# Six joined edits to a fused attention, mLSTM and GLA layer: opening, value products, first output sums, y splits, last tile, weight buffers

## The chip, the core and the metric

The kernel runs on one core of a Trainium2 chip. TensorE (PE in the rows, PEld for its weight loads) multiplies into PSUM banks, VectorE (DVE), ScalarE (ACT) and GpSimd (POOL) work element by element, and SyncE (SP) issues nearly all DMAs. The metric is the device time of one execution in microseconds, the median of the runs.

## What is computed

One layer over 2048 tokens of width 1024, in fp32. `h` is the RMS norm of `x`; one input projection feeds three head groups, whose gated outputs are concatenated and projected back, with a residual and a final RMS norm:

```
hn = rmsnorm(x, norm_g);  z = hn @ w_in        # split into aq ak av ag | mq mk mv mo mi mf mg | gq gk gv ga gg
y_a = band_chunk_attention(aq, ak, av, rel_bias) * silu(ag)     # 6 heads of 64, own 64-chunk + 8 previous
y_b = sigmoid(mo) * head_rmsnorm(mlstm(conv(mq), conv(mk), mv, mi, mf)) * silu(mg)     # 6 heads of 64
y_c = head_rmsnorm(gla(gq, gk, gv, log_alpha(ga))) * silu(gg)   # 4 heads, keys 32, values 64
out = rmsnorm(x + concat(y_a, y_b, y_c) @ w_out, final_g)
```

## The kernel before, in words

Every large product is made of fp32r operands split in two: `hi` is the value rounded by a ScalarE copy (line 237 for weights, 332 for `x`, 997 for `y`), `lo` the rest by a subtraction on VectorE or GpSimd (238, 333, 998); three matmuls (hi hi, hi lo, lo hi) make one product. The 2048 tokens go in four quarters of 512.

**The opening.** `prep_x` (283) loads the quarter's `x` token by token, squares it with a row sum on ScalarE, and makes diagonal tiles `dg` of the norm factors; `prep` (297) multiplies them by ones on TensorE (302) so that the factors stand along the free axis, copies them to SBUF (`rbs`, 304), loads `xT` (feature-major `x`), scales it in place on VectorE (311), and multiplies the small gate weights `wg` (318). `split_x` (326) makes the eight `X` tiles. Only then does the first projection `proj_z` (436, matmuls at 245 to 247) start.

**Phase A.** Per quarter: `proj_z` (gq, gk), `proj_t` (258, values, token-major), gg, mq/mk with a convolution, mo/mg, and the nine attention projections; between them stand the pieces of the mLSTM (`mlstm`), of GLA (`gla_in`, `gla`) and of the gates. TensorE's order is the program's, written by a planner (`Flow`) with estimated gaps; the other engines' and SP's orders come from the framework's scheduler. Weight tiles `w` are split from raw loads in two `wraw` buffers into a ring of five. Attention's q, k, v and gates and the finished mLSTM and GLA outputs go to DRAM (`q_d`, `k_d`, `v_d`, `ga_d`, `y_d`). Of the last quarter's attention projections six tiles are kept back (`kept`).

**Phase B.** `attention0` runs the first quarter's six heads: `scores` (936; matmuls at 960, `pt` the probabilities) and `mix` (1001). It runs beside the kept projections. `load_wo` splits the output weights and loads and splits the first quarter's `y` tiles 3 to 7. In `mix` the probabilities of each pair of 128-token tiles are transposed (1032) in packs of up to 512 columns, split into `ph` and `pl` (1037, 1038), and multiplied with the values `vv` (1046 hi, 1049 lo), two packs behind; the sum in the one bank `w` goes to `cc` (1052, 1053), and after each second head `split_y` makes y tiles 0 to 2. Then, for quarters 1 to 3, `attention(q)` is merged with `out_mm(q - 1)` (1088; matmuls 1099 to 1101, order of the y tiles 3, 4, 5, 6, 7, 0, 1, 2); the quarter's y tiles 3 to 7 come back from DRAM by `load_y` (1119). `out_mm(3)` runs alone at the end, and each of its tiles ends in residual add, square sum, gain, norm factor and store (1104 to 1116).

Of the kernel before, what the change touches and what calls it, by code (L numbers as in the profile page):

```python
# [8 lines left out]
FP32 = mybir.dt.float32  # L9
# [18 lines left out]
G0 = 96  # L28

# [46 lines left out]
def merge(a, b, na, nb):  # L76
    acc = 0
# [27 lines left out]
def trunk_kernel(ctx: ExitStack, tc: tile.TileContext, xT, x, w_f, w_t, w_o, w_gates, norm_g, conv_w,  # L105
# [34 lines left out]
    wring = pg_.enter_context(tc.tile_pool(name="wring", bufs=5))  # L140
# [3 lines left out]
    with ExitStack() as pa_:  # L144
# [13 lines left out]
        def d_tile():  # L158
# [18 lines left out]
        zr = d_tile()  # L177
        nc.gpsimd.memset(zr, 0.0)
        nc.vector.tensor_copy(hl_nm, zr.rearrange("p h t -> p (h t)")[:, 0:QT])
        nc.vector.tensor_copy(hl_iw, zr[:, 0, 0:NC])  # L180
        nc.gpsimd.affine_select(out=zr[0:32], in_=zr[0:32], pattern=[[-1, 6], [0, P]], compare_op=ALU.not_equal,
                                fill=1.0, base=0, channel_multiplier=1)
        nc.scalar.copy(zr[32:64], zr[0:32])
        nc.scalar.copy(zr[96:128], zr[0:32])
        nc.vector.memset(zr[0:32], 0.0)
        nc.vector.tensor_copy(sel, zr)
# [33 lines left out]
        def load_consts():  # L220
            nc.sync.dma_start(wg[:, :, 0:28], w_gates)
            nc.sync.dma_start(onerow, one_row)
            nc.sync.dma_start(gsel, gate_sel)
# [6 lines left out]

        def load_w(src, k):
            w = wring.tile([P, 2 * D], FR, name="w").rearrange("p (k l n) -> p k l n", k=k, l=2)
# [8 lines left out]
        def proj_g(name, X, out_, per):  # L241
            w = load_w(w_f[_F.index(name)], KT)
# [40 lines left out]
        def prep_x(q):  # L283
            t0 = q * QT
            rs = big.tile([P, NC], FP32, name="rs")
            for tt in range(NC):
                xt = xraws.tile([P, D], FP32, name="xraw")
                nc.sync.dma_start(xt, x[t0 + tt * P:t0 + (tt + 1) * P, :])
                nc.scalar.activation(xt, xt, AF.Square, accum_out=rs[:, tt:tt + 1])
# [7 lines left out]
        def prep(q, R, dg):  # L297
# [26 lines left out]
            R["raws"], R["g1"] = raws, g1  # L324

# [11 lines left out]
        def gates(q, g1, R):  # L337
# [26 lines left out]
            nc.scalar.copy(hl_nm[G0:G0 + MH], nm)  # L364
# [12 lines left out]
            nc.scalar.copy(hl_iw[G0:G0 + MH], il)  # L377
# [136 lines left out]
        def proj_kept(X):  # L514
            for b, name in kept:
                out_ = []
                yield from proj_g(name, X, out_, 1)
                att_in(NQ - 1, X, b, out_[0])

        def bias_rel():  # L520
            bc = big.tile([P, AH], FP32, name="sm")
            nc.sync.dma_start(bc, bias[:, :, 256])
            for p in range(AH // 2):
                b2 = g_tile([P, QT]).rearrange("p (h j) -> p h j", h=2)
                nc.sync.dma_start(b2, bias[:, 2 * p:2 * p + 2, 0:256])
                for h in range(2):
                    nc.gpsimd.tensor_scalar(b2[:, h, :], b2[:, h, :], bc[:, 2 * p + h:2 * p + h + 1], None, op0=ALU.subtract)
# [701 lines left out]
```

## Time and profile before

| what | value |
|---|---|
| median of 3 runs | 1318.02 us (1317.06 to 1320.14) |
| profiled execution | 1321.42 us, of it 1319.7 us span from first to last instruction |
| TensorE busy | 1266.8 us, 96% of the span |
| VectorE, ScalarE, GpSimd busy | 813.0, 595.9, 630.6 us |
| mean granted TensorE clock | 0.982 |

Busy time of TensorE counts overlapping matmuls once, and a matmul that runs at half clock is as busy as one at full clock, so 96% does not say how much is left. What is left shows as waits of TensorE and as stretches of granted clock 0.5. In the timeline a matmul's own duration is longer than its share of the stream; its price is the distance from its start to the next one's.

### The profile page before, as it was taken

The numbers are of one execution on the slowest core, as the hardware profiler recorded it, in microseconds if no ns is written. First come the engines' busy times: TensorE is split into PE (matmuls) and PEld (weight loads), VectorE is DVE, ScalarE is ACT, GpSimd is POOL, SyncE is SP. The second block draws the span as 40 slices with busy tenths as digits, with TensorE's granted clock in tenths as the row PEclk, the third lists the DMA queues.
The fourth block names the chain that finished last, engine by engine and source line by source line (L and its number), as shares of the span: only waits on it lengthen the run. The fifth ranks groups of instructions, "written<-read, shape, count | busy, mean of one in ns | idle before, by whom it ended". The sixth has DMA issues, their size and how long they took to land.

```text
span 1319.7 us, 19935 instructions
## 1 busy us (share of the span) xinstructions
PE 1266.8 (96%) x7044; PEld 1038.1 (79%) x7044; DVE 813.0 (62%) x1859; ACT 595.9 (45%) x1124; POOL 630.6 (48%) x847
## 2 busy tenths in 40 slices
PE   4999999999999999999999999999979999999997
PEld 2788777878787788877778787887768888889876
DVE  7626656672775767267666866664467767666711
ACT  5624422463443247244224543332466556556621
POOL 5327652332766225367622656642165454454442
PEclk7999999999999999999999999999889999999999
DMA  7444233634423354442244333328677656565222
GB/s 249 157 120 136 84 104 113 181 121 138 129 80 106 111 183 133 127 134 86 91 127 125 112 102 88 108 69 260 180 221 218 184 176 187 157 206 148 81 95 79
DMA packets 106516, 181.66 MB, mean 138 GB/s; under 512 B 9776, under 2 KB 54704, under 8 KB 106416
## 3 DMA queue, kind: packets, MB, share of 16 engines
q1 hardware_dynamic: 101808, 172.00, 43.6%
q10 hardware_dynamic: 4608, 8.39, 1.7%
q8 instruction: 55, 0.90, 0.3%
q14 instruction: 45, 0.37, 0.1%
HBM read 143.92 MB, written 36.44 MB: 137 GB/s over the span
## 4 chain that ended last, share of the span: by engine, by line
PE 81%; DVE 8%; DMA 3%; ACT 3%; issue 2%; POOL 2%; SPq 1%; POOLq 0%; DVEq 0%; ACTq 0%
PE ip L245 13%; PE ip L247 12%; PE ip L246 12%; PE ip L1101 4%; PE ip L1099 4%; PE ip L1100 4%; PE ip L265 3%; PE s L960 3%; PE ip L267 3%; PE ip L266 3%; PE tp L1032 3%; PE w L1049 2%; PE w L1046 2%; PE ga L748 2%; PE s L600 1%
## 5 line engine op out<-in xcount | busy, mean ns | idle before, releaser
L245 PE MATMUL ip<-x,w 128*128 128x512 f32 x800 | 329.2, 412 | 0.0
L247 PE MATMUL ip<-x,w 128*128 128x512 f32 x800 | 314.4, 393 | 0.0
L246 PE MATMUL ip<-x,w 128*128 128x512 f32 x800 | 313.6, 392 | 0.0
L245 PEld LDWEIGHTS ip<-x,w 128*128 128x128 f32 x800 | 151.3, 189 | 42.0 <-issue 12.9
L247 PEld LDWEIGHTS ip<-x,w 128*128 128x128 f32 x800 | 150.9, 189 | 33.4
L246 PEld LDWEIGHTS ip<-x,w 128*128 128x128 f32 x800 | 151.5, 189 | 29.0 <-issue 2.2
L238 DVE TENSOR_TENSOR w<-wraw,w 128x1024 fp32r<-128x1024 f32 x88 | 122.8, 1395 | 70.0 <-ACT w L237 64.2
L237 ACT CAST w<-wraw 128x1024 fp32r<-128x1024 f32 x132 | 137.9, 1046 | 60.4 <-DMA wraw<-in_w_f 27.6
L238 POOL TENSOR_TENSOR w<-wraw,w 128x1024 fp32r<-128x1024 f32 x44 | 107.8, 2449 | 79.3 <-ACT w L237 79.3
L981 POOL TENSOR_SCALAR pt<-pt,sm 128x640 f32<-128x640 f32 (+2 forms) x96 | 71.2, 743 | 135.8 <-DVE sm L980 110.5
L265 PE MATMUL ip<-w,x 128*128 128x512 f32 x256 | 101.9, 398 | 4.9 <-ACT vg L429 4.7
L267 PE MATMUL ip<-w,x 128*128 128x512 f32 x256 | 99.9, 390 | 0.0
L266 PE MATMUL ip<-w,x 128*128 128x512 f32 x256 | 99.8, 390 | 0.0
L979 ACT ACTIVATE pt<-pt,sm 128x640 f32<-128x640 f32 (+2 forms) x96 | 73.3, 763 | 52.9 <-DVE sm L976 51.8
L691 POOL TENSOR_TENSOR prd<-gk,zg 128x16 f32<-128x16 f32 (+7 forms) x112 | 66.1, 590 | 60.6 <-PE pw L697 55.2
L960 PE MATMUL s<-kk,qq 128*128 128x256 f32 (+2 forms) x360 | 83.9, 320 | 5.7 <-DMA kk<-k_d 2.4
L1038 DVE TENSOR_TENSOR pl<-tp,ph 128x512 fp32r<-128x512 f32 (+2 forms) x126 | 73.9, 597 | 22.8 <-ACT ph L1037 21.5
L1037 ACT CAST ph<-tp 128x512 fp32r<-128x512 f32 (+2 forms) x126 | 63.1, 512 | 41.8 <-PE tp L1032 37.9
L400 ACT ACTIVATE e<-ip 128x512 f32<-128x512 f32 x44 | 26.1, 593 | 122.6 <-PE ip L247 106.3
L960 PEld LDWEIGHTS s<-kk,qq 128*128 128x128 f32 x360 | 63.5, 198 | 16.1 <-issue 5.2
L688 POOL TENSOR_TENSOR gk<-gk,al 128x16 f32<-128x16 f32 (+14 forms) x120 | 71.2, 594 | 8.5 <-ACT al L665 1.3
L470 DVE SCALAR_TENSOR_TENSOR qk<-u,cw,qk 128x512 f32<-128x512 f32 x72 | 69.7, 969 | 8.9 <-ACT qk L468 7.5
(303 smaller groups left out, 2544.8 us busy)
## 6 DMA issues: line engine op xcount, KB each, us to landing
wraw<-in_w_f SPq DMA_DIRECT2D x100, 512.0 KB, 3.6
wraw<-in_w_t SPq DMA_DIRECT2D x32, 512.0 KB, 3.7
qq<-q_d SPq DMA_DIRECT2D x48, 256.0 KB, 5.8
kk<-k_d SPq DMA_DIRECT2D x18, 512.0 KB, 6.8
vv<-v_d SPq DMA_DIRECT2D x18, 512.0 KB, 4.9
xraw<-in_x SPq DMA_DIRECT2D x16, 512.0 KB, 5.9
xraw<-in_xT SPq DMA_DIRECT2D x16, 512.0 KB, 6.8
xr<-in_x SPq DMA_DIRECT2D x16, 512.0 KB, 3.6
```

The source lines that it names most:

```text
L237: nc.scalar.copy(w[:, :, 0, :], rv)
L238: other().tensor_tensor(w[:, :, 1, :], rv, f32(w[:, :, 0, :]), op=ALU.subtract)
L245: nc.tensor.matmul(ps, w[:, k, 0, :], X[k][:, 0, :], start=(k == 0), stop=False)
L246: nc.tensor.matmul(ps, w[:, k, 0, :], X[k][:, 1, :], start=False, stop=False)
L247: nc.tensor.matmul(ps, w[:, k, 1, :], X[k][:, 0, :], start=False, stop=(k == KT - 1))
L265: nc.tensor.matmul(ps, X[k][:, 0, t], w[:, 0, :], start=(k == 0), stop=False)
L266: nc.tensor.matmul(ps, X[k][:, 0, t], w[:, 1, :], start=False, stop=False)
L267: nc.tensor.matmul(ps, X[k][:, 1, t], w[:, 0, :], start=False, stop=(k == KT - 1))
L688: nc.gpsimd.tensor_tensor(b16(gk)[:, :, 0:c], b16(gk)[:, :, 0:c], b16(al)[:, :, c:c + 1].broadcast_to([P, NB, c]), op=ALU.mult)
L960: nc.tensor.matmul(sp[:, :cn], qq[:, l, tt * P:(tt + 1) * P], kk[:, ko + c0:ko + c0 + cn], start=(l == 0), stop=(l == 1))
L979: nc.scalar.activation(pt[:, :n], pt[:, :n], AF.Exp, bias=init, scale=-1.0, accum_out=sm[:, 2:3])
L1038: nc.vector.tensor_tensor(pl[:, :wd], tp[:, :wd], f32(ph[:, :wd]), op=ALU.subtract)
```

## The change

1. **Opening.** `prep_first` replaces `prep_x`, `prep`, `split_x` and `proj_z` for quarter 0: it loads `xT` first, squares it on ScalarE, sums over features by matmuls with a column of ones, and scales from the PSUM bank `rb`; the loads and most instructions are pinned in program order. gq and gk run interleaved by feature block, the products with `X` lo last, the gate product between. The first four value weights are loaded into the `qk` and `gg` tiles and split ahead. Constants for `sel`, `hl_nm`, `hl_iw` are made later.
2. **Value products.** `mix` handles all four token tiles at once: one matmul per key block over up to 512 columns, five full packs a head (three in quarter 0).
3. **Partial output sums.** The first ten steps of `out_mm(0)` (y tiles 3 to 7, both halves of the first tile) stand beside the last heads of quarter 0; `load_wo` is spread over the last four kept tiles.
4. **y splits.** `load_y` subtracts on VectorE for odd tiles, GpSimd for even; from quarter 1 on `out_mm` takes the y tiles in the order 0, 1, 3, 4, 5, 6, 7, 2.
5. **Last tile.** Its second half leaves out the separate gain product on GpSimd; its halves are stored from SP and ACT.
6. **Buffers and moves.** Six `w` and two `u` buffers; kept weights loaded up to five ahead; `prep_x` of the next quarter after `proj_m`, its loads pinned in SP's order; two copies of `gates` go from ACT to DVE, the bias subtraction from POOL to ACT.

```
+        def prep_first():
...
+                    raw = xraws.tile([P, 2, QT], FP32, name="xraw")
+                    pin(nc.sync.dma_start(raw, xT[:, 2 * g:2 * g + 2, 0:QT]))
...
+                for g in range(4):
+                    sq = sqs[g % 2].rearrange("p (a t) -> p a t", a=2)
+                    pin(nc.scalar.activation(sq, raws[g], AF.Square))
+                    pin(nc.vector.tensor_tensor(sq[:, 0, :], sq[:, 0, :], sq[:, 1, :], op=ALU.add))
+                    for tt in range(NC):
+                        nc.tensor.matmul(ss[:, tt:tt + 1], sq[:, 0, tt * P:(tt + 1) * P], ones[:, 0:1],
...
+                hi(ws[0])
+                hi(ws[1])
+                lo(nc.vector, ws[0])
...
+                    pin(nc.vector.tensor_scalar(dg[:, tt, :], ident, rs[:, tt:tt + 1], None, op0=ALU.mult))
+                    nc.tensor.matmul(rb[:, tt * P:(tt + 1) * P], ones, dg[:, tt, :], start=True, stop=True)
+                lo(nc.vector, ws[1])
...
+                    op = pin(nc.vector.scalar_tensor_tensor(rk[k], rk[k], ng[:, k:k + 1], rb, op0=ALU.mult, op1=ALU.mult))
+                    pin(nc.scalar.copy(X[k][:, 0, :], rk[k]))
...
+                nc.tensor.matmul(ps[0], wq[:, k, 0, :], X[k][:, 0, :], start=(k == 0), stop=False)
+                nc.tensor.matmul(ps[0], wq[:, k, 1, :], X[k][:, 0, :], start=False, stop=False)
+                nc.tensor.matmul(ps[1], wk[:, k, 0, :], X[k][:, 0, :], start=(k == 0), stop=False)
...
+            use = [[tt for tt in range(NC) if pts[tt][1] <= b < pts[tt][1] + pts[tt][2]] for b in range(nkb)]
+            packs = ([2, 0], [1, 6], [3], [4], [5, 7]) if q else ([0], [1, 3], [2])
...
-                yield from merge(a, b, 8, 14)
+                yield from merge(a, b, 8, 10, -12)
...
+                order = (3, 4, 5, 6, 7, 0, 1, 2) if q == 0 else (0, 1, 3, 4, 5, 6, 7, 2)
...
-            Y[k] = split_y(raw, q, k)
+            Y[k] = split_y(raw, q, k, nc.vector if k % 2 else nc.gpsimd)
...
+        when = [KT * (len(kept) - 4) + n for n in (3, 6, 11, 19, 22, 27)]
...
+        parts, left = out_mm(0, YA), 10
+        for i, _ in enumerate(first):
+            next(wl, None)
+            if left and i >= 8 and i % 2 == 0:
+                next(parts)
+                left -= 1
```

TensorE's first rows before: warm-up products, the norm factors (`pw<-g,ones`), the gate product (`pw<-xraw,wg`), then gq (`ip<-x,w`).

```order
L156 MATMUL pw<-ones 128x128 x14
L302 MATMUL pw<-g,ones 128x512
L318 MATMUL pw<-xraw,wg 32x512 x8
L245 MATMUL ip<-x,w 128x512
L246 MATMUL ip<-x,w 128x512
```

TensorE's first rows now; `ga` is the square sum, `gb` the bank `rb` of norm factors.

```order
L157 MATMUL pw<-ones 128x128 x14
L379 MATMUL ga<-ones,vg 128x1 x4
L379 MATMUL ga<-ones,zg 128x1 x4
L388 MATMUL pw<-ones 128x128 x3
L393 MATMUL gb<-g,ones 128x128 x4
L396 MATMUL pw<-ones 128x128 x2
L415 MATMUL ip<-x,w 128x512
L416 MATMUL ip<-x,w 128x512
L417 MATMUL ip<-x,w 128x512
```

The gate product has moved behind gq and gk, and the rows of the square sum are new.

TensorE before, between the last heads of quarter 0, after the kept projections: value products (`w<-ph,vv`, `w<-pl,vv`), scores (`s<-kk,qq`) and transposes (`tp<-ident,pt`).

```order
L1049 MATMUL w<-pl,vv 64x256 x2
L960 MATMUL s<-kk,qq 128x384 x2
L1032 MATMUL tp<-ident,pt 128x128 x6
L960 MATMUL s<-kk,qq 128x256 x2
L1032 MATMUL tp<-ident,pt 128x128 x4
L960 MATMUL s<-kk,qq 128x384 x2
L1046 MATMUL w<-ph,vv 128x128
L1046 MATMUL w<-ph,vv 128x256
```

TensorE now at the same place; `ip<-w,y` are the partial output sums.

```order
L1157 MATMUL w<-pl,vv 64x256
L1078 MATMUL s<-kk,qq 128x384 x2
L1209 MATMUL ip<-w,y 128x512
L1210 MATMUL ip<-w,y 128x512
L1211 MATMUL ip<-w,y 128x512
L1138 MATMUL tp<-ident,pt 128x128 x8
L1209 MATMUL ip<-w,y 128x512
L1210 MATMUL ip<-w,y 128x512
L1211 MATMUL ip<-w,y 128x512
L1078 MATMUL s<-kk,qq 128x256 x2
L1138 MATMUL tp<-ident,pt 128x128 x2
```

Output products stand now between the last value product of one head and the first of the next.

GpSimd before, at the end of the last head of quarter 3: gate product (`cc<-cc,gt`), y splits, and the gain and norm factor of output tiles (`xr<-xr,e`, `mhalf`).

```order
L1067 TENSOR_TENSOR cc<-cc,gt 128x512
L998 TENSOR_TENSOR y<-wraw,y 128x512
L1107 TENSOR_TENSOR xr<-xr,e 128x512
L998 TENSOR_TENSOR x<-cc,x 128x512
L998 TENSOR_TENSOR y<-wraw,y 128x512 x2
```

GpSimd now at the same place.

```order
L1116 TENSOR_TENSOR y<-wraw,y 128x512
L1174 TENSOR_TENSOR cc<-cc,gt 128x512
L1116 TENSOR_TENSOR x<-cc,x 128x512
L1228 TENSOR_TENSOR xr<-xr,e 128x512
L1116 TENSOR_TENSOR y<-wraw,y 128x512
```

Three of the five splits of loaded y tiles have left GpSimd for VectorE.

## Rows read from the trace of the kernel before

**Rows 1.** The page: busy time of the engines, their shares of the span, and the instructions.

```profile
PE 1266.8 (96%) x7044; PEld 1038.1 (79%) x7044; DVE 813.0 (62%) x1859; ACT 595.9 (45%) x1124; POOL 630.6 (48%) x847
```

**Rows 2.** Busy time by stretch: start and end, length, then busy time (instructions) of PE, PEld, DVE, ACT, POOL, granted clock, DMA share and GB/s.

```profile
940.00:970.00 30.00, 30.00 (x177) 25.82 (x175) 14.44 (x51) 14.20 (x34) 9.92 (x13) 1.00 0.48 129
970.00:1003.00 33.00, 24.86 (x143) 21.96 (x142) 27.32 (x68) 25.59 (x54) 24.47 (x21) 0.79 1.01 303
```

**Rows 3.** TensorE's waits over the whole span: who waited, for whom, us in total, times, longest.

```profile
PE pw L302 <- DVE g L294: 9.4, 1, 9.4
PE w L1049 <- DVE pl L1038: 5.5, 6, 2.7
...
PE ip L265 <- ACT vg L429: 4.7, 4, 2.1
PE w L1046 <- DVE cc L1053: 2.8, 1, 2.8
...
PE s L960 <- DMA kk<-k_d: 2.4, 1, 2.4
...
PE ip L1099 <- ACT y L997: 2.0, 1, 2.0
PE ip L1101 <- POOL y L998: 1.7, 2, 1.1
```

**Rows 4.** Busy time in stretches of granted clock 0.5, columns as in rows 2.

```profile
9.20:26.10 16.90, 5.18 (x11) 1.41 (x12) 11.01 (x17) 10.11 (x16) 6.30 (x5) 0.50 0.93 301
...
975.10:981.90 6.80, 5.84 (x27) 5.14 (x27) 4.67 (x15) 4.68 (x11) 4.59 (x6) 0.50 1.01 344
985.40:992.10 6.70, 4.98 (x23) 4.88 (x24) 4.72 (x13) 3.19 (x8) 4.37 (x4) 0.50 1.07 339
```

**Rows 5.** Timeline of the opening: start, duration, engine, line, what, count, and idle time before it with its releaser.

```profile
4.44 1.04 ACT L237 CAST w<-wraw 128x1024 fp32r<-128x1024 f32 x1 [2.37 <-DMA wraw<-in_w_f]
5.73 1.04 ACT L237 CAST w<-wraw 128x1024 fp32r<-128x1024 f32 x1 [0.25 <-DMA wraw<-in_w_f]
...
14.03 1.03 POOL L291 TENSOR_TENSOR rs<-rs,mhalf 128x4 f32<-128x4 f32 x1 [3.08 <-DVE rs L290]
...
15.09 0.87 DVE L294 TENSOR_SCALAR g<-ident,rs 128x128 f32<-128x128 f32 x4 [1.15 <-POOL rs L291]
15.88 1.22 DVE L238 TENSOR_TENSOR w<-wraw,w 128x1024 fp32r<-128x1024 f32 x1
...
20.42 6.77 DVE L311 SCALAR_TENSOR_TENSOR xraw<-xraw,ng,g 128x512 f32<-128x512 f32 x6 [3.32 <-ACT g L304]
...
27.22 0.62 ACT L332 CAST x<-xraw 128x512 fp32r<-128x512 f32 x1 [1.06 <-DVE xraw L311]
...
31.75 0.50 PE L245 MATMUL ip<-x,w 128*128 128x512 f32 x1
...
34.61 1.02 PE L340 MATMUL pw<-g,gsel 128*128 128x512 f32 x2
35.07 0.79 PE L245 MATMUL ip<-x,w 128*128 128x512 f32 x1
...
44.53 0.39 PE L265 MATMUL ip<-w,x 128*128 128x512 f32 x1
44.75 0.39 PE L266 MATMUL ip<-w,x 128*128 128x512 f32 x1
```

**Rows 6.** Timeline of TensorE in quarter 2's attention: one scores step of 384 columns, and the value products of packs of two singles and a double, of two doubles, and of one double.

```profile
1126.31 0.40 PE L1046 MATMUL w<-ph,vv 128*128 128x256 f32 x2
1126.54 0.40 PE L1049 MATMUL w<-pl,vv 128*64 128x256 f32 x2
1126.78 0.51 PE L960 MATMUL s<-kk,qq 128*128 128x384 f32 x2
1127.12 0.28 PE L1046 MATMUL w<-ph,vv 128*128 128x256 f32 x1
...
1138.39 0.50 PE L1046 MATMUL w<-ph,vv 128*128 128x128 f32 x3
1138.73 0.40 PE L1049 MATMUL w<-pl,vv 128*64 128x128 f32 x3
1138.97 0.41 PE L1046 MATMUL w<-ph,vv 128*128 128x256 f32 x2
```

**Rows 7.** Timeline of VectorE and GpSimd while the output weights are split.

```profile
971.34 0.68 DVE L406 SCALAR_TENSOR_TENSOR e<-e,ip 128x512 f32<-128x512 f32 x1
971.75 1.27 POOL L932 TENSOR_TENSOR y<-wraw,y 128x512 fp32r<-128x512 f32 x1
...
972.78 1.31 DVE L932 TENSOR_TENSOR w<-xr,w 128x1024 fp32r<-128x1024 f32 x1
...
983.16 2.36 POOL L932 TENSOR_TENSOR w<-wraw,w 128x1024 fp32r<-128x1024 f32 x1
983.55 3.05 DVE L932 TENSOR_TENSOR w<-xr,w 128x1024 fp32r<-128x1024 f32 x1
```

**Rows 8.** Timeline of the last output tile's end.

```profile
1313.54 1.26 POOL L1107 TENSOR_TENSOR xr<-xr,e 128x512 f32<-128x512 f32 x1 [4.27 <-ACT jk L1106]
...
1314.76 0.55 POOL L1112 TENSOR_TENSOR sm<-sm,mhalf 128x1 f32<-128x1 f32 x1
1315.34 0.72 ACT L1115 ACTIVATE xr<-xr,sm 128x512 f32<-128x512 f32 x1 [1.88 <-POOL sm L1112]
```

More of the change, by code (lines that the diff above doesn't have):

```diff
@@ L514, in proj_kept @@
         def proj_kept(X):
-            for b, name in kept:
+            ws = []
+            for i, (b, name) in enumerate(kept):
+                while len(ws) < min(i + 5, len(kept)):
+                    ws.append(load_w(w_f[_F.index(kept[len(ws)][1])], KT))
                 out_ = []
-                yield from proj_g(name, X, out_, 1)
+                yield from proj_g(name, X, out_, 1, ws[i])
                 att_in(NQ - 1, X, b, out_[0])
@@ L849, in trunk_kernel @@
             flow.need("mlstm")
+            qk = proj_m(X)
             dg = prep_x(q + 1)
-            qk = proj_m(X)
             flow.need("gates")
@@ L1038, in turn_ @@
[L1038 to L1053 removed]
+                nc.scalar.copy(ph[:, :w], tp[:, :w])
@@ new lines, in turn_, with to, pv @@
+                nc.vector.tensor_tensor(pl[:, :w], tp[:, :w], f32(ph[:, :w]), op=ALU.subtract)
+                for b in pk:
+                    src[b] = ph[:, src[b]], pl[:, src[b]]
+            def to(b, r=slice(0, P)):
+                return op[r, use[b][0] * P:use[b][0] * P + P * len(use[b])]
+            def pv(pk):
+                for b in pk:
+                    nc.tensor.matmul(to(b), vv[:, b, :], src[b][0], start=not done, stop=False, skip_group_check=True)
+                    done.append(b)
+                for b in pk:
+                    nc.tensor.matmul(to(b, slice(0, 64)), vv[:, b, 64 * (h % 2):64 * (h % 2) + 64], src[b][1],
+                                     start=False, stop=(len(done) == nkb and b == pk[-1]), skip_group_check=True)
@@ L1055, in mix @@
             held = []
-            for it in todo:
-                ph, pl = turn_(*it)
+            for pk in packs:
+                turn_(pk)
                 yield
-                held.append(it + (ph, pl))
+                held.append(pk)
                 if len(held) > 2:
-                    pv(*held.pop(0))
+                    pv(held.pop(0))
                     yield
-            pv(*held.pop(0))
+            pv(held.pop(0))
             yield
-            pv(*held.pop(0))
+            pv(held.pop(0))
@@ L1128, in trunk_kernel @@
         wl = load_wo(YA)
+        when = [KT * (len(kept) - 4) + n for n in (3, 6, 11, 19, 22, 27)]
         for i, _ in enumerate(proj_kept(X)):
             next(first, None)
-            if i >= KT * len(kept) - 6:
+            if i in when:
                 next(wl)
-        for _ in first:
+        parts, left = out_mm(0, YA), 10
+        for i, _ in enumerate(first):
             next(wl, None)
+            if left and i >= 8 and i % 2 == 0:
+                next(parts)
+                left -= 1
         run_all(wl)
+        for _ in range(left):
+            next(parts)
         for q in range(1, NQ):
```

240 lines of the change are left out of this document (162 added, 78 removed).

## The prediction

> **What bounds the kernel now.** I read the page first, then TensorE's waits, then busy time by stretch, then the timeline where the waits lie. TensorE is busy 96% of the span, the next engine 62% [rows 1]: the matmul stream sets the time, and an edit pays only where that stream stands still, runs at half clock, or gets shorter. Three places stand out. In the opening TensorE waits 9.4 us for the norm factors [rows 3], and the first projection matmul starts at 31.75 [rows 5]. At the end of quarter 0's attention, 970 to 1003, TensorE is busy 24.86 of 33 us at a mean clock of 0.79 [rows 2], while all of 940 to 970 is full. At the last quarter's end the output product waits for y tiles (2.0 and part of 1.7 us, [rows 3]). The rest are small waits, many of which the change does not touch. The sum is made on the profiled execution, 1321.42 us (span 1319.7, so 1.7 lie around it); it is 3.4 above the median of the three runs, 1318.02, and I take the difference off the median.
>
> **Opening.** Before, value weights start at 44.53, after two gate products of which each costs 0.9 us (two instructions, start to start 0.46, and a similar delay of the next matmul, [rows 5]); without them the same point is 42.7. Now: a load of 512 KB is ready at 4.44, 3.6 us after the queue starts, and the next 1.29 later [rows 5]. `xT` stands behind one tiny load, so its four loads are ready near 4.9, 6.2, 7.5 and 8.8, the gq and gk weights at 10.1 and 11.4. Square of the last (1.04, as the cast of that size), the add of two halves (0.7) and the ones-products (estimated 1 to 2 us, from 0.46 for a fp32 pair at full clock) end near 12.3; VectorE meanwhile splits gq. Then the power on GpSimd 1.03, the diagonals 0.87, the last product about 0.4, the gk split 1.22, which stands ahead of the scaling: 15.9. The scalings come 0.66 apart, each cast takes 0.62, so the first `X` is there at 17.2 instead of 31.75. From there TensorE has 32 matmuls of 0.227 (start to start of 44.53 and 44.75 is 0.22), eight gate pairs of 0.46 and 16 matmuls again: 7.3 + 3.7 + 3.6 = 14.6, if at full clock. The opening before ran at granted clock 0.5 from 9.2 to 26.1 [rows 4]; I charge 5 us of matmuls at half clock, 2.5 us lost: values start at 34.2. Gain 42.7 - 34.2 = **8.5**. If half clock lasts through all 24 matmuls that follow the scalings, or the scalings are stretched, 5; without half clock, 11.
>
> Stretching is where a rule is weighed. Before, six scalings took 6.77 us, 1.13 each, with GpSimd at work beside them [rows 5], and a weight split took 3.05 instead of 1.31 when GpSimd's split of 2.36 had started just ahead of it; a scaling of one SBUF operand and one PSUM operand took 0.68 although GpSimd started a split during it [rows 7]. The Trainium skill, "SBUF — State Buffer", section "Who interferes with whom", says the same in general: VectorE with two SBUF inputs and GpSimd that reads SBUF block each other, with one SBUF input they don't. By that rule the new scalings, which read the factors from PSUM, are not stretched, while the y splits that go to VectorE may be; these three rows agree. The sum uses 0.66; at 1.13 each it would be 3.8 us later at the eighth `X`, which is the low bound above.
>
> **Value products.** A head of quarters 1 to 3 has two pairs of tiles, each with a pack of two singles and a double, one of two doubles and one double. From start to start [rows 6]: 0.34 + 0.24, 0.23 + 0.24, and 0.12 hi and about as much lo, 1.29 a pair, 2.58 a head. Now there are eight blocks of widths 1, 2, 3, 4, 4, 3, 2, 1. Singles cost 0.11 hi and 0.06 lo (what is left of the first pack beside its double at 0.12), doubles 0.12, triples 0.175 (two scores of 384 columns take 0.34), fours 0.227: hi 1.26, lo 1.16, together 2.43. That is 0.15 a head and **2.7** for 18 heads; quarter 0 gives nearly nothing. The number of transposes stays. Casts and subtractions fall from six to five a head, off the path. Fewer packs mean fewer chances to wait for `pl`; I add **1.3** for these and take 4.0 (bounds 1 and 6.5, the upper with nearly all small waits of the quarters gone).
>
> **Partial output sums and earlier output weights.** In 900 to 1003 the waits for `pl` (5.5 in all, nearly all here) and `cc` (2.8) [rows 3] and two half-clock stretches with 5.84 and 4.98 us of matmuls [rows 4], half of which is loss, make 8 + 5.4 = 13.4 us. Their cause is in rows 7: the `cc` add and `pl` stand on VectorE behind output-weight splits of 1.31 and 3.05. The change starts these splits during the kept projections, where VectorE is busy 14.4 of 30 us and the DMAs 0.48 [rows 2], and puts ten steps of 3 x 0.23 = 6.9 us of TensorE work between the heads. That work is only moved and gains nothing by itself; it is cover. But 970 to 1003 is also full on the DMAs (1.01) and VectorE (27.3 of 33), so not all moves. I take 60%: **8** (bounds 3 and 12). The waits of the first scores for `kk` (2.4, [rows 3]) stay: the same bytes are queued ahead of these loads on SP.
>
> **y splits and order.** At the end of quarter 3, GpSimd has the gate product, five splits and the gains in one queue. Now three splits are VectorE's, and the stream starts with tiles 0 and 1, which are ready, and ends with tile 2. The waits there are 2.0 and about 0.6, followed by a short half-clock stretch: up to 5 us. Tile 6 still stands behind tile 2's split and a gain on GpSimd (1.3 us each, as in [rows 8]) and may be late by some 1.5 us. Gain **3** (bounds 0 and 5).
>
> **Last tile.** The power waits for a gain product of 1.26 that leaves the path [rows 8]; a power that follows an idle GpSimd took 1.03 rather than 0.55 [rows 5]. So 0.4 there and about 0.5 by two store queues: **0.9** (bounds 0 and 1.3).
>
> **Buffers and moves.** `prep_x` moved behind `proj_m` puts four squares of about 1.25 into ScalarE's queue between the convolution's copies, and the next quarter's loads behind the weights on SP; the norm-factor product comes far later in TensorE's order, so both are covered. If the cover fails, each quarter pays up to 2 us where banks wait for ScalarE. Two copies leave ScalarE's gate chain, behind which value tiles wait 4.7 us in all [rows 3]. The bias subtraction on ScalarE and the second `u` buffer lie beside full matmul streams. A sixth `w` buffer meets no wait of the stream. **0.5** (bounds -3 and +3).
>
> **Sum.** 8.5 + 4.0 + 8 + 3 + 0.9 + 0.5 = 24.9, so 1318.0 - 24.9 = 1293.1: forecast **1293**.
>
> **Rivals.** (a) *The stall stays, only later.* The partial sums need `wo` and y tiles 3 to 7 split; if these are late on VectorE, TensorE waits at them instead. For: 970 to 1003 is full on three resources. Against: the splits are started about 25 matmul groups earlier. Item three shrinks to its bound of 3: 1298. (b) *The opening is paced by VectorE and half clock:* low bound 5, 1296.6. For: 16.9 us of clock 0.5 before, and the scalings stand behind two weight splits. Against: the PSUM operand. (c) *The phase switch heals too:* with kept weights loaded early, the first `kk` loads land sooner and the half-clock stretches around them go, some 5 us more, and the third item is near its upper bound: 1285. Against: bytes ahead are the same. (d) *Slower:* every pack is now 512 wide, so `ph` and `pl` take ScalarE and VectorE longer, and the value product waits for `pl` in steady state. There are 18 x 5 = 90 such packs; the point from which this decides is 24.9 / 90 = 0.28 us each; at 0.4 the time is 1318.0 - 24.9 + 36 = 1329. Against: the packs are two behind, and before only few of the packs waited at all. The same sign would need tens of us from the later `x` loads, which have most of a quarter's stream as cover.
>
> **How the numbers follow.** Forecast (1288 to 1296) 0.57; (a) 0.14; (b) 0.12; (c) 0.13; (d) 0.04. The cases other than (d) lie between 1281 and 1304 with the bounds of single terms, which seldom all fall to one side; that leaves out less than 2 in 10. A measurement can tell about 0.2% (2.6 us) from no change: faster than that 0.95, within it 0.02, slower 0.03.
>
> **What would show it.** First matmul of gq near 17 and first value matmul near 34 in the timeline; no wait over 1 us for `pl` or `cc` at the end of quarter 0 and granted clock 1.0 there; value products near 2.4 us a head, start to start; waits for y under 2 us before the last output product; store of the last tile about 7 us after the last matmul. The forecast is wrong if the quarters of phase A, 60 to 900, no longer take the same time, if partial sums wait for `y` or `w`, or if `pl` waits appear in every head.

## The result and the profile after

The changed kernel takes 1310.93 us (median of 4 runs, 1308.93 to 1311.46) against 1318.06 of the kernel before (1317.06 to 1320.14): ratio 0.9941, 95% interval 0.9924 to 0.9958. It gained 7.1 us where 25 were forecast. The two profiled executions differ by more, spans of 1319.7 and 1307.2 us: that of before was slower than all four of its runs, that of after the fastest of its four. So the pair shows some 5 us more than the medians, and I use it for where time went, the ratios for how much.

The page: TensorE's busy share has hardly moved, from 96% [rows 1] to 97%, with 120 matmuls fewer.

```profile
PE 1267.8 (97%) x6924; PEld 1035.1 (79%) x6924; DVE 807.6 (62%) x1866; ACT 592.2 (45%) x1098; POOL 601.4 (46%) x829
```

Three marks cut the span into stretches that every kernel here has: the first and the last matmul of the value projections (`proj_t`, in phase A), and the last matmul of all. The view of one source line gives them: durations, then "first to last start". Before:

```profile
L265 PE MATMUL ip<-w,x x256: 389/389/505, 44.5 to 832.8; 128*128 128x512 f32 x128
...
L1101 PE MATMUL ip<-x x32: 388/392/397, 1093.0 to 1311.5; 128*128 128x512 f32 x32
```

After:

```profile
L261 PE MATMUL ip<-w,x x256: 387/389/798, 32.0 to 826.1; 128*128 128x512 f32 x128
...
L1221 PE MATMUL ip<-x x32: 388/393/398, 1076.2 to 1299.6; 128*128 128x512 f32 x32
```

The first mark comes 12.5 us earlier. From first to last value projection it is 788.3 before and 794.1 now: 5.8 are given back, of which 1.8 are the two gate products that now stand behind the first mark. From there to the last matmul it is 478.7 and 473.5: 5.2 gained, where the value products, partial sums and y splits were to bring 15. What follows the last matmul shrinks from 8.2 to 7.6.

The opening's rows after (timeline; those of before are [rows 5]): gq starts at 18.81, not at 31.75, and all eight scalings take 5.36, 0.67 each, although GpSimd starts a split at 20.81.

```profile
17.35 5.36 DVE L401 SCALAR_TENSOR_TENSOR xraw<-xraw,ng,gb 128x512 f32<-128x512 f32 x8 [0.45 <-PE gb L393]
...
18.81 0.52 PE L415 MATMUL ip<-x,w 128*128 128x512 f32 x1 [0.64 <-ACT x L402]
...
20.81 1.30 POOL L408 TENSOR_TENSOR x<-xraw,x 128x512 fp32r<-128x512 f32 x1 [5.95 <-ACT x L402]
...
22.62 4.12 DVE L408 TENSOR_TENSOR x<-xraw,x 128x512 fp32r<-128x512 f32 x2
...
26.81 2.48 DVE L408 TENSOR_TENSOR x<-xraw,x 128x512 fp32r<-128x512 f32 x4
```

The first two subtractions behind them, with two SBUF inputs beside a busy GpSimd, take 2.06 each; the next four, with GpSimd idle from 26.2 on, 0.62 each. Both agree with the rule of the Trainium skill that the prediction weighed ("SBUF — State Buffer", "Who interferes with whom").

TensorE's waits after; `vg`, `dr` and `at` lie in phase A, `kk`, `pl`, `sm` (row sums of the probabilities), `ph`, `y` at the phase switch and behind it:

```profile
PE s L1078 <- DMA kk<-k_d: 5.9, 2, 3.0
PE w L1157 <- DVE pl L1145: 3.4, 5, 2.2
PE s L1078 <- DVE sm L1094: 3.0, 4, 1.1
PE w L1154 <- ACT ph L1144: 2.6, 3, 1.1
PE ip L261 <- ACT vg L547: 2.6, 2, 1.4
PE ip L1221 <- POOL y L1116: 2.6, 2, 1.6
PE gb L866 <- ACT dr L823: 2.2, 1, 2.2
PE ga L887 <- DVE at L880: 1.7, 1, 1.7
PE ip L1219 <- ACT y L1115: 1.5, 1, 1.5
```

Against [rows 3], the 9.4 for the norm factors and the 2.8 for `cc` are gone, `pl` is down from 5.5, and `dr` and a wait for `y` at 994 are new; `at`, `ph` and `sm` are up from 0.5, 0.3 and 1.3. `kk` is up from 2.4 by the view, but TensorE waited twice there before too; the first time, 2.0 at 916, the view gives no releaser:

```profile
PE s L960 <- issue: 2.0, 1, 2.0
```

So these two waits together rise from 4.4 to 5.9. Busy time by stretch, columns as in [rows 2]:

```profile
940.00:970.00 30.00, 28.27 (x153) 23.46 (x152) 20.24 (x62) 20.20 (x45) 15.45 (x18) 0.96 0.76 216
970.00:1003.00 33.00, 28.27 (x144) 23.57 (x144) 24.52 (x58) 19.43 (x42) 18.06 (x17) 0.88 0.85 247
...
356.80:360.20 3.40, 3.40 (x11) 2.73 (x10) 2.61 (x4) 1.86 (x3) 3.01 (x10) 0.50 0.47 154
595.80:602.60 6.80, 6.80 (x26) 4.96 (x25) 5.36 (x13) 3.06 (x5) 1.48 (x2) 0.50 0.21 55
...
995.10:998.50 3.40, 3.07 (x11) 2.79 (x12) 1.38 (x2) 1.32 (x4) 0.32 (x2) 0.50 0.73 205
```

The end of quarter 0 is fuller (28.27 of 33 at clock 0.88, before 24.86 at 0.79 [rows 2]), but 940 to 970 is no longer full (the stream is 6.7 us ahead at the second mark, so the same times do not hold quite the same work). Two half-clock stretches stand in phase A, where the kernel before had none. TensorE's waits of over 0.2 us in phase A come to 7.4 us before and 8.7 now; the half clock, 10.2 us of it, is the larger part of what phase A lost.

The first of them starts so (timeline): ScalarE idles 4.01 us for the convolution on VectorE, a weight cast follows, and only then the copy `dr` that TensorE has waited 2.18 for. ScalarE was free, but its queue is in order.

```profile
352.72 0.63 ACT L590 ACTIVATE e<-qk 128x512 f32<-128x512 f32 x1 [4.01 <-DVE qk L588]
353.26 0.57 ACT L579 COPY u<-ip 128x512 f32<-128x512 f32 x1
353.73 1.05 ACT L232 CAST w<-wraw 128x1024 fp32r<-128x1024 f32 x1
354.67 0.37 ACT L823 COPY dr<-pw 128x256 f32<-128x256 f32 x1
...
355.10 0.33 PE L866 MATMUL gb<-ident,dr 128*128 128x128 f32 x1 [2.18 <-ACT dr L823]
```

The new wait for y: the partial sums have used up tiles 3 to 7, two products take tiles 0 and 1, and the next needs y tile 2, whose head has just ended; its cast and its subtraction are waited for one after the other.

```profile
993.09 0.61 ACT L1115 CAST y<-cc 128x512 fp32r<-128x512 f32 x1
...
993.76 0.50 PE L1219 MATMUL ip<-x,y 128*128 128x512 f32 x1 [1.54 <-ACT y L1115]
...
994.11 1.27 POOL L1116 TENSOR_TENSOR y<-cc,y 128x512 fp32r<-128x512 f32 x1
...
995.43 0.80 PE L1221 MATMUL ip<-x,y 128*128 128x512 f32 x1 [0.94 <-POOL y L1116]
```

### The profile page after: what moved, and what is told of

Read it like the earlier page. It is cut to its first block, busy times and chain, and to the rows that moved or that the text cites. A ratio compares the mean times of both kernels' runs of the same rounds, so it can differ in the third digit from the quotient of the medians.

```text
span 1307.2 us, 19535 instructions
## 1 busy us (share of the span) xinstructions
PE 1267.8 (97%) x6924; PEld 1035.1 (79%) x6924; DVE 807.6 (62%) x1866; ACT 592.2 (45%) x1098; POOL 601.4 (46%) x829
## 4 chain that ended last, share of the span: by engine, by line
PE 76%; DVE 7%; POOL 5%; ACT 4%; DMA 4%; issue 3%; SPq 0%; POOLq 0%; ACTq 0%; DVEq 0%
PE ip L241 11%; PE ip L242 10%; PE ip L243 10%; PE ip L1219 4%; PE ip L1221 4%; PE ip L1220 4%; PE ip L261 3%; PE ip L263 3%; PE ip L262 3%; PE s L1078 3%; PE tp L1138 3%; DVE qk L588 2%; PE ga L870 2%; PE w L1154 2%; PE s L722 2%
## 5 line engine op out<-in xcount | busy, mean ns | idle before, releaser
L241 PE MATMUL ip<-x,w 128*128 128x512 f32 x784 | 322.9, 412 | 1.1 <-ACT vg L547 0.8
L243 PE MATMUL ip<-x,w 128*128 128x512 f32 x784 | 308.6, 394 | 0.0
L242 PE MATMUL ip<-x,w 128*128 128x512 f32 x784 | 308.5, 393 | 0.0
L241 PEld LDWEIGHTS ip<-x,w 128*128 128x128 f32 x784 | 148.9, 190 | 42.6 <-issue 12.5
L243 PEld LDWEIGHTS ip<-x,w 128*128 128x128 f32 x784 | 148.7, 190 | 32.7
L242 PEld LDWEIGHTS ip<-x,w 128*128 128x128 f32 x784 | 149.2, 190 | 28.4 <-issue 1.9
L233 POOL TENSOR_TENSOR w<-wraw,w 128x1024 fp32r<-128x1024 f32 x42 | 102.8, 2448 | 117.9 <-ACT w L232 109.3
L232 ACT CAST w<-wraw 128x1024 fp32r<-128x1024 f32 x126 | 131.6, 1046 | 40.7 <-DMA wraw<-in_w_f 24.6
L233 DVE TENSOR_TENSOR w<-wraw,w 128x1024 fp32r<-128x1024 f32 x84 | 114.4, 1363 | 57.6 <-ACT w L232 57.3
L1145 DVE TENSOR_TENSOR pl<-tp,ph 128x512 fp32r<-128x512 f32 (+1 forms) x108 | 72.0, 672 | 35.5 <-ACT ph L1144 35.2
L1144 ACT CAST ph<-tp 128x512 fp32r<-128x512 f32 (+1 forms) x108 | 60.4, 572 | 41.6 <-PE tp L1138 40.4
L810 POOL TENSOR_TENSOR gk<-gk,al 128x16 f32<-128x16 f32 (+14 forms) x120 | 67.7, 564 | 22.4 <-ACT al L787 14.5
```

The costliest lines, as they stand in the source:

```text
L232: nc.scalar.copy(w[:, :, 0, :], rv)
L233: other().tensor_tensor(w[:, :, 1, :], rv, f32(w[:, :, 0, :]), op=ALU.subtract)
L241: nc.tensor.matmul(ps, w[:, k, 0, :], X[k][:, 0, :], start=(k == 0), stop=False)
L242: nc.tensor.matmul(ps, w[:, k, 0, :], X[k][:, 1, :], start=False, stop=False)
L243: nc.tensor.matmul(ps, w[:, k, 1, :], X[k][:, 0, :], start=False, stop=(k == KT - 1))
```

## Experiments

The ratio is to the kernel before on the same chip; the last three columns are of each kernel's profiled execution: first value projection, from it to the last one (phase A), and from there to the last matmul (us). Where the opening is new, phase A holds the 1.8 us of the two gate products as well.

| kernel | ratio (95%) | first | phase A | rest |
|---|---|---|---|---|
| before | 1 | 44.5 | 788.3 | 478.7 |
| changed | 0.9941 (0.9924 to 0.9958) | 32.0 | 794.1 | 473.5 |
| item 1 alone | 1.0017 (1.0006 to 1.0029) | 33.5 | 797.1 | 480.7 |
| item 2 alone | 1.0037 (1.0023 to 1.0051) | 43.6 | 788.6 | 486.0 |
| item 3 alone | 1.0064 (1.0050 to 1.0078) | 45.2 | 788.5 | 492.1 |
| item 3, six `w`, early kept loads | 1.0047 (1.0029 to 1.0066) | 44.6 | 793.2 | 477.4 |
| items 1 and 6 | 1.0000 (0.9984 to 1.0016) | 31.6 | 794.2 | 482.3 |
| all but 1 | 1.0076 (1.0048 to 1.0105) | 44.4 | 797.3 | 476.3 |
| all but 2 | 0.9932 (0.9916 to 0.9948) | 32.7 | 794.5 | 473.8 |
| all but 3 | 0.9988 (0.9974 to 1.0002) | 31.5 | 794.1 | 480.6 |
| all but 4 | 0.9932 (0.9911 to 0.9953) | 33.9 | 794.0 | 475.2 |
| all but 5 | 0.9926 (0.9907 to 0.9945) | 31.5 | 794.2 | 473.6 |
| all but most of 6 | 0.9958 (0.9942 to 0.9973) | 34.6 | 795.8 | 473.0 |
| `prep_x` back | 0.9910 (0.9895 to 0.9926) | 34.7 | 793.6 | 471.8 |
| GLA later | 0.9933 (0.9919 to 0.9946) | 34.1 | 795.4 | 474.1 |
| first y later (Y) | 0.9897 (0.9880 to 0.9913) | 31.8 | 791.5 | 471.8 |
| Y, bias table later | 0.9894 (0.9877 to 0.9910) | 33.6 | 794.1 | 469.5 |
| Y, third `kk` | 0.9908 (0.9893 to 0.9923) | 33.9 | 796.8 | 471.0 |
| Y, `prep_x` back | 0.9900 (0.9881 to 0.9918) | 32.7 | 793.2 | 472.0 |
| Y, old value products | 0.9942 (0.9927 to 0.9958) | 31.9 | 793.8 | 478.9 |

### One item alone

**Item 1** on the kernel before, with the six `w` buffers that it needs.

```
-        flow.start("prep", prep(0, R, prep_x(0)))
...
+        g1, X, z = prep_first()
+        flow.start("gates", gates(0, g1, R))
```

> The kernel before with item 1 alone (the new opening, and the six w buffers that it needs). In the changed kernel's trace the first value matmul starts 12.5 us earlier than before, but only 6.4 of it are left at 750 us. Theory A, what was gained is lost again by other items (the moves of item 6): the opening alone keeps about 11, so 1307, ratio 0.9915, and the distance to the kernel before stays 10 to 12 us from 60 to 900. Theory B, the opening's gain melts by itself, since the other engines' work in phase A does not come earlier by as much: about 6, so 1312, ratio 0.9955, the loss at the same places (355, 504, 595 us). The prediction's step: 8.5, so 1309.5.

Theory B, and worse: all is lost. TensorE's waits in this kernel (`qk` and `g` are conv and gate work of phase A):

```profile
PE ip L261 <- ACT vg L547: 3.8, 3, 2.9
PE s L695 <- DVE qk L591: 3.0, 1, 3.0
...
PE pw L465 <- ACT g L462: 2.0, 1, 2.0
```

The kernel before has none of these at 256, 508 and 800. The one at 508 has the same form as `dr` above, the copy `vg` behind an instruction that waited 2.20 for VectorE:

```profile
507.36 0.42 ACT L793 ACTIVATE lc<-lc 128x256 f32<-128x256 f32 x1 [2.20 <-DVE lc L792]
507.68 0.47 ACT L545 ACTIVATE v<-ip 128x384 f32<-128x384 f32 x1
508.05 0.26 ACT L547 COPY vg<-ip 128x128 f32<-128x128 f32 x1
```

**Item 2** on the kernel before.

```
-                yield from merge(a, b, 8, 14)
+                yield from merge(a, b, 8, 10, -12)
```

(with the new `mix`.) 

> The kernel before with item 2 alone (value products over four tiles, five full packs a head, merged with the scores 8 to 10). The prediction's step: 4.0 gained, so 1314.0, ratio 0.9970. What the two traces show, if the other items do nothing there: the quarters 1 to 3 came 2.2 us closer together, so 1316, ratio 0.9983. A rival: value products that wait for the full packs eat the shorter stream, no gain, 1318, ratio 1.000.

Slower by more than the rival allowed: phase A is that of before, the rest is 7.3 longer. TensorE's waits for `ph` are 9.5 us in four. One, at the joint of two quarters:

```profile
1084.15 0.40 PE L1038 MATMUL w<-pl,vv 128*64 128x512 f32 x1
1085.91 0.62 ACT L996 CAST y<-wraw 128x512 fp32r<-128x512 f32 x1 [5.79 <-DMA wraw<-y_d]
1086.43 0.58 ACT L1025 CAST ph<-tp 128x512 fp32r<-128x512 f32 x1
...
1087.07 0.50 PE L1035 MATMUL w<-ph,vv 128*128 128x512 f32 x1 [2.52 <-ACT ph L1025]
```

ScalarE idled 5.79 for a DMA: the cast of the next quarter's loaded y tile stands in its queue ahead of the cast of `ph`. That the shorter stream arrives there earlier and the load does not is my reading; no run tests it.

**Item 3** on the kernel before, then with six `w` buffers and the kept weights loaded up to five ahead.

```
+        when = [KT * (len(kept) - 4) + n for n in (3, 6, 11, 19, 22, 27)]
...
+            if left and i >= 8 and i % 2 == 0:
+                next(parts)
```

> The kernel before with item 3 alone: ten partial output sums beside the last heads of quarter 0, and the output weights loaded over the last four kept tiles. The prediction's step: 8 gained, 1310 to 1312, ratio 0.994. By the changed kernel without it, 6.2: ratio 0.995. A rival: with the old opening and value products the switch has other waits, and the earlier loads push the first kk back, so that it gains 2 or less, ratio 0.9985 or more.

> The kernel before with item 3, the six w buffers and the early loads of kept weights from item 6. Item 3 alone was 8.4 us slower (ratio 1.0064): TensorE stood 9.3 us at 972 and 1.8 us at 955 for a kept projection's weight tile, behind output weights in the same ring. Theory A: item 3 needs the early loads, which take exactly these waits: they go, and of the 6.9 us of moved sums 3 to 6 are gained, ratio 0.9955 to 0.998. Theory B: with the old value products and opening the switch finds other waits for the same weights and splits: 1.000 or more.

Item 3 alone: a kept projection stands 9.28 us for its weight tile. Its load was issued on SP only at 967.69, behind output weights and attention loads, and its cast is ready at 972.5.

```profile
967.69 0.33 SPq L235 DMA_DIRECT2D wraw<-in_w_f  x1
...
971.42 1.04 ACT L237 CAST w<-wraw 128x1024 fp32r<-128x1024 f32 x1 [4.69 <-DMA wraw<-in_w_f]
...
972.52 0.80 PE L245 MATMUL ip<-x,w 128*128 128x512 f32 x1 [9.28 <-ACT w L237]
```

With the early loads this wait is gone and the rest falls from 492.1 to 477.4: item 3 needs that part of item 6. But the ratio is still above 1, since phase A took 4.9 us longer with the ring of six and the early loads. So theory A holds for the wait, theory B for the time.

The early loads stand behind phase A in the program, and nothing else in phase A differs between these two kernels but the sixth buffer and a smaller DMA scratch that makes room for it. With five buffers (item 2 alone, item 3 alone) every engine works in the order of the kernel before until 896 us. With six, ScalarE casts two weight tiles at 28 us where it cast one, ahead of two `x` casts, and from there on the orders of ScalarE, VectorE, GpSimd and SP are others. ScalarE before, and with six:

```profile
27.75 1.04 ACT L237 CAST w<-wraw 128x1024 fp32r<-128x1024 f32 x1
...
27.82 1.99 ACT L237 CAST w<-wraw 128x1024 fp32r<-128x1024 f32 x2
```

### The joined change without one item

**Items 1 and 6 alone; all but item 1; all but most of item 6** (`prep_x`, the `u` buffer, gate copies and bias subtraction as before):

```
-            z = proj_z(X) if q else z
+            z = proj_z(X)
```
```
+            dg = prep_x(q + 1)
             qk = proj_m(X)
-            dg = prep_x(q + 1)
...
-                zb = big.tile([P, 3 + QT], FP32, name="u", bufs=2)
+                zb = big.tile([P, 3 + QT], FP32, name="u", bufs=1)
```

> The kernel before with items 1 and 6 alone. In the changed kernel the two together leave 6.4 us at 900. Theory C: the phase switch then takes back part of it, since the kk loads and the output weights do not come earlier by as much: the opening alone lost 2.2 us from 808 to 1010, so 1312 to 1314, ratio 0.9955 to 0.997. Theory D: it keeps all 6.4, 1311.6 or less, ratio 0.995. Theory E: all is taken back as in the opening alone, 1318 or more, ratio 1.000.

> The changed kernel with the opening of before (items 2 to 6 stay). The opening alone brought nothing (ratio 1.0017), and in its trace stalls stood at 256, 508 and 800 us that the kernel before lacks. Theory C: the moves of item 6 only take away stalls that the earlier start brings, so without the new opening they are worth nothing, phase A runs as in the kernel before, and this is 6 us slower than the changed kernel, 1317, ratio 0.999. Theory D: the moves have a gain of their own of some 4 us, and the opening is worth the other 2: 1313, ratio 0.996. Theory E: the opening is worth nothing in the changed kernel either: 1311, ratio 0.994.

> The changed kernel with the moves of item 6 undone but the six w buffers and the early loads of kept weights: prep_x again before proj_m with unpinned loads, one u buffer, the two copies of the gate chain on ScalarE, the bias subtraction on GpSimd. Theory A, the moves cost what phase A gives back: 5 us faster than the changed kernel, 1306, and the distance to the kernel before at 750 us is about 11.5 instead of 6.4. Theory B, the opening's gain melts by itself: 1311, the same as the changed kernel. The prediction's step: 0.5 slower.

Items 1 and 6 bring nothing together: theory E by time, though phase A's part of the gain reaches its end. Without item 1 the rest is 10 us slower than the kernel before, worse than every theory: phase A takes 797.3, since stalls for `dr`, `at` and `vg` of 1.2 to 2.2 us appear there too. So in the joined change the opening is worth (1.0076 - 0.9941) x 1318 = 18 us (12 to 24 by the intervals), where alone it was worth nothing. In the third run theory A falls: without the moves phase A is no shorter (795.8), so they do not cost what phase A gives back. Its time, 2 us longer, cannot be told from theory B or from the prediction's 0.5.

**All but items 2, 3, 4, 5.**

```
+                order = (3, 4, 5, 6, 7, 0, 1, 2)
-                order = (3, 4, 5, 6, 7, 0, 1, 2) if q == 0 else (0, 1, 3, 4, 5, 6, 7, 2)
...
-            Y[k] = split_y(raw, q, k, nc.vector if k % 2 else nc.gpsimd)
+            Y[k] = split_y(raw, q, k, nc.gpsimd)
```
```
-                final = q == NQ - 1 and tt == NC - 1
+                final = False
```

(items 4 and 5; 2 and 3 put back `mix`, and the loop over `first`.) 

> The changed kernel with the value products of before (pairs of tiles, merged 8 to 14). Alone, item 2 cost 5.4 us, by waits for ph at the joints of heads and quarters. Theory C: the partial sums fill those joints, so here item 2 keeps what the shorter stream gives, 2 to 4 us: 1313 to 1315, ratio 0.996 to 0.998. Theory D: item 2 costs its 5 us here too: 1306, ratio 0.991. The prediction's step: 4.0, so 1315.

> The changed kernel without item 3: no partial output sums beside the last heads, and the output weights loaded from the last six steps of the kept projections on, as before. The prediction's step: 8 lost, so 1319, the same as before. Theory from the two traces: the stretch 900 to 1003 has no net gain in the changed kernel, so this is within 2 us of it, 1309 to 1313, with the waits for pl and cc back and those for y at the first output product gone. A rival: the earlier splits and sums cost more than they bring, and this is 2 or more us faster, 1309 or less.

> The changed kernel without item 4: all five splits of loaded y tiles on GpSimd, y tiles in the order 3 to 7, 0, 1, 2. The prediction's step is 3.0, and the two traces show 3.7 at the last junction: 1314 to 1315, ratio 0.9965 to 0.9975, with the wait at the last output product back to 2 us or more and half clock after it. A rival: the waits of the last junction are worth no more than they measure, about 1 us in all: 1312, ratio 0.995.

> The changed kernel without item 5: the last tile ends as the others do. The prediction's step is 0.9; the spans after the last matmul differ by 0.4 in the two traces: 0.4 to 0.9 slower than the changed kernel, ratio 0.9944 to 0.995. A rival, by the rows of the kernel before: 0, ratio 0.994.

Item 3 is worth (0.9988 - 0.9941) x 1318 = 6.2 us (2 to 10 by the intervals), near the forecast and against the theory that I had formed from the two traces. Items 2, 4 and 5 cannot be told from nothing: leaving them out gave 0.9926 to 0.9932. For item 2 the intervals exclude the 4.0 of the prediction.

### The stalls by themselves

**GLA later.** Two of the planner's gaps raised.

```
-                yield 0.0, 2.0
+                yield 0.0, 5.0 if held is None else 2.0
...
-                    yield 1.2, 6.0 if held is None else 4.5
+                    yield 1.2, 8.5 if held is None else 4.5
```

> The changed kernel with two of the planner's gaps for GLA raised (2 to 5 us ahead of the transposes of dr and kd, 6 to 8.5 us ahead of the products with at), so that TensorE's order has these pieces some four to six matmul groups later. Theory A: what phase A gives back of the opening is the stalls at 355 (2.2 us, then half clock to 360) and at 595 (1.7 us, then half clock to 603): they go, the distance to the kernel before at 800 us grows from 6.6 to some 11, and this is 4 to 5 us faster than the changed kernel, ratio 0.990 to 0.991. Theory B: what is lost in phase A is not a matter of these two places; other pieces then wait in their stead, and the time is that of the changed kernel, ratio 0.994.

Theory A falls. The stalls at 355 and 595 are gone, others stand in their place, and phase A takes 795.4:

```profile
PE mt L662 <- DVE m L760: 3.1, 1, 3.1
...
PE ip L261 <- ACT vg L547: 1.9, 1, 1.9
PE ip L1219 <- ACT y L1115: 1.5, 1, 1.5
PE s L699 <- DVE dd L692: 1.3, 1, 1.3
```

**`prep_x` back** ahead of `proj_m`, the rest as changed. 

> The changed kernel with prep_x again ahead of proj_m, its loads unpinned; the rest of item 6 stays. All the moves of item 6 put back cost about 2 to 4 us. Theory A: prep_x carries that: the wait of 2.9 us for vg at 508 comes back, those at 355 and 595 go, and this is 2 to 4 us slower than the changed kernel, ratio 0.995 to 0.997. Theory B: the gate copies and the u buffer carry it, and prep_x only trades one stall for two: the same or up to 3 us faster, ratio 0.991 to 0.994.

Theory B by time, but its interval touches that of the changed kernel; the waits trade places as theory A said (2.9 at 510, none at 355 and 595).

**First y later (Y).**

```
+            nb = YN - (q == 1) * 10
+            run_all(merge(attention(q, YB, nxt), om, units * 10 + 8 * (units - 1), nb, -7 * nb if q == 1 else 0))
```

> The changed kernel in which quarter 1's attention gets eight steps ahead of the first output product that needs y tiles 0 to 2. In the changed kernel this product waited 1.5 and 0.9 us at 994 to 995, and half clock followed to 998.5. If these are lost time of their own, this is 3 to 4 us faster, ratio 0.991 to 0.992. A rival: the steps that are put ahead wait themselves, for ph, pl or sm, since no output product lies between them any more: no change, ratio 0.994, with waits of 1 us or more at 994 to 1003.

It holds, with a part for the rival: 0.9897, about 4 to 6 us faster than the changed kernel and its neighbours in the table. The waits for y at 994 are gone; one for `pt` has come:

```profile
993.18 0.76 PE L1138 MATMUL tp<-ident,pt 128*128 128x128 f32 x5 [1.81 <-POOL pt L1099]
...
994.48 0.45 PE L1219 MATMUL ip<-x,y 128*128 128x512 f32 x1
```

In its profile 1.7 us are gained behind phase A and 2.6 in phase A, whose program is the same: there the stall at 595 was not followed by half clock this time. So the size in its own place is nearer to 2 by the profile than to the 4 of the ratio; the two do not agree closer.

**Y with one more edit:** the bias table loaded behind the first `kk`; three `kk` buffers; `prep_x` back; the old value products.

```
-        nc.sync.dma_start(bt, b_d)
...
+            if q == 0 and h == 0:
+                dma.dma_start(bt, b_d)
```
```
+            kk = early.tile([P, 1024], FR, name="kk", bufs=3)
```

> The kernel with quarter 1's first output product later (ratio 0.9897), and the bias table of the attention loaded behind the first head's kk instead of ahead of it. Theory A: the first scores wait for kk (2.6 us at 907, half clock to 912) because of the bytes queued ahead, of which the table is 768 KB: the kk load lands 2 to 3 us earlier, wait and half clock go, 2 to 4 us faster, ratio 0.987 to 0.988. Theory B: the load cannot be issued earlier, or the scores' next step waits for the table on VectorE: no change, 0.990.

> The kernel with quarter 1's first output product later (ratio 0.9897), and three kk buffers instead of two. Theory A: the wait of 4.3 us for kk at 924 and the half clock around it (922 to 929) come from the third head's load, which is issued only when the first head's buffer is free: with a third buffer it is issued ahead, and 4 to 6 us are gained, ratio 0.985 to 0.987. Theory B: the queues are full there and the same bytes only land in another order: the wait moves to the first kk or to weights, no change, 0.990.

> The changed kernel with two of the edits tried so far: quarter 1's first output product eight attention steps later (alone 0.9897), and prep_x ahead of proj_m with unpinned loads (alone 0.991). Theory A, the waits of the two places are apart and add up: 0.987. Theory B: what prep_x changes in phase A is taken up before the phase switch, so only the first edit counts: 0.990.

> The changed kernel with quarter 1's first output product later (alone 0.9897), and the value products of before. Theory A: item 2 is worth nothing in the joined change, as the run with the old value products said (0.9932 against 0.9941): 0.989 to 0.990. Theory B: with the attention steps ahead of the output product, the joint that item 2 makes longer is bare, and the old value products are 2 to 4 us faster: 0.987. Theory C: the shorter stream of item 2 shows once the wait for y is gone: 2 to 4 us slower, 0.992.

Theory B in the first three. With the table later the first wait for `kk` goes and the second grows from 4.3 to 7.0; with three buffers the first grows from 2.6 to 4.3, and one of 3.0 for `qq` stands in place of the second. With the old value products the kernel is 0.0045 x 1318 = 6 us slower (2 to 10 by the intervals): theory C. So no version is clearly faster than Y, 0.9897.

## Why the prediction was wrong

Two steps failed: phase A was taken as unchanged, and the savings behind it were summed as if the waits would not come back in other places. By the profiled pair, whose spans differ by 12.5:

- **Opening**, forecast 8.5 (5 to 11): in its own place 44.5 - 1.8 - 32.0 = 10.7. Half clock ended at 18.9, as the stream began, so the 2.5 charged for it was not due; the gate pairs took 1.85 and not 3.7, and the stream began at 18.81 and not at 17.2. The 1.13 for a stretched scaling was a mean: four of those six took 0.66. Rival (b) falls. The step was right and somewhat small.
- **Buffers and moves**, forecast 0.5 (-3 to +3): this step failed. Of the moves the text said "so both are covered", of the buffer "A sixth `w` buffer meets no wait of the stream"; it named a changed phase A as a sign of being wrong, and its sum took phase A as unchanged. Phase A lost 5.8 - 1.8 = 4.0, by the half clock behind two stalls more than by the stalls. In the three kernels with a ring of five `w` buffers phase A takes 788.3 to 788.6; in the seventeen with six it takes 791.5 to 797.3 (1.8 of it the gate products where the opening is new). It stays long whichever item is left out: the opening (797.3), the moves (795.8), items 2 to 5 (794.0 to 794.5); and item 1 alone has no early loads. So the sixth buffer, with the DMA scratch cut for it, is all that the seventeen share, and it changes the order in every queue that fills the ring. That it is the cause is not shown: no run has the sixth buffer and nothing else, and none the whole change with five. Taking away two stalls brought others; why these and not others appear stays open.
- **Value products** 4.0, **partial sums** 8, **y splits** 3: 15 forecast, 5.2 found: these terms failed together, and by the larger part, 9.8. Behind phase A the waits that they were to save came back elsewhere: those of over 0.2 us come to 19.4 us before and 20.3 now, while half clock fell from 27.2 us to 17.1. The partial sums were right in size (6.2 by ratio, 7.1 in the last stretch; forecast 8, 3 to 12): between 960 and 1003 half clock holds 20.4 us without them and 10.2 with them. But they brought a wait of their own, y tile 2 at 994, 2.5 us and half clock. It is of the kind that rival (a) named, but at tile 2 and not at 3 to 7. It was missed because the steps were counted (ten) and not what the steps right behind them need.
- The value products' stream did get shorter: behind 1010 us a head's products take 2.43 us from start to start, as forecast, against 2.69 before (2.58 by the text), 4.3 over 17 heads. In the time it shows as 6 (2 to 10) with the later output product and as nothing without it. Alone they cost 4.9, by waits for `ph` behind y casts in ScalarE's queue. That is near rival (d), but at joints and not in each head: "only few of the packs waited at all" was true of heads and was not asked of joints. What they are worth in the joined change stays open between 0 and the forecast.
- y splits: not told from 0 by the ratio, 1.7 by the profile. At the last output product a wait of 1.6 for GpSimd's split stays, near the 1.5 that the text allowed for tile 6.
- The waits for `kk` did not "stay": the text priced one of 2.4, the two came to 4.4 before, and to 6.3 with items 1 and 6 and 7.5 with item 1 alone. The last stretch is longer there by 3.6 (482.3) and 2.0. Against 482.3, items 2 to 5 gain 8.8 (473.5); so 3.6 of the missing 9.8 went here.
- **Last tile** 0.9: 0.6 behind the last matmul, nothing by ratio. The text misread a row: the power took 1.03 for four columns [rows 5] and 0.55 for one [rows 8], and with one column behind an idle GpSimd it still takes 0.55:

```profile
1302.07 0.55 POOL L1233 TENSOR_TENSOR sm<-sm,mhalf 128x1 f32<-128x1 f32 x1 [4.73 <-DVE sm L1232]
```

Sum: 10.7 - 4.0 - 3.6 + 8.8 + 0.6 = 12.5, against 24.9: the opening 2.2 over its forecast, phase A 4.5, the switch and the quarters 9.8, and the last tile 0.3 under theirs. The rest to 7.1 is the distance of the two profiled executions from their medians.

## What to carry to other kernels

A gain at the front of an in-order pipeline is worth what later meetings let through: cost not only the edit, but each place behind it where the fastest engine can now arrive too early, and what stands ahead of the awaited instruction in the other engines' queues. Items that move work need a list of what the next instructions after the moved ones read. A further buffer is no free room either: it may change the order of every queue that fills it, so it wants a run by itself. And items can be a unit: one, two and three were each slower alone, by 2 to 8 us, and all six together were faster; a test of one at a time would have refused them all.

## What the runs showed of the hardware

Half clock followed waits, and cost about as much as they did. Over the twenty profiled executions, between 60 and 900 us, 24 of 28 waits of TensorE of 2 us or more and 10 of 16 of 1.5 to 2 us were followed by granted clock 0.5; none of some 110 waits of 0.3 to 1.5 us was, and no half clock came there without such a wait. The stretches lasted 3.4 us (24 times) or 6.8 (10 times). Products of 512 columns stand 0.43 us apart in one and 0.23 behind it, here in the changed kernel at clock 0.5 and, from 360.2 on, at 1.0:

```profile
358.34 0.63 PE L241 MATMUL ip<-x,w 128*128 128x512 f32 x1
358.76 0.63 PE L242 MATMUL ip<-x,w 128*128 128x512 f32 x1
...
360.59 0.39 PE L241 MATMUL ip<-x,w 128*128 128x512 f32 x1
360.82 0.40 PE L242 MATMUL ip<-x,w 128*128 128x512 f32 x1
```

So nearly half of such a stretch is lost, and by that estimate a stall of 2.2 costs 2.2 + 1.7 = 3.9 or 2.2 + 3.4 = 5.6. Which it is differs between executions whose phase A is the same program (behind the stall at 595, 6.8 us in the changed kernel, none in Y), and that may be part of why single profiles differ by some us.
